# A hybrid decoder of two layers on one core: two buffers instead of one for the packed parameter tiles of a layer

## The chip, the cores and the metric

The kernel runs on one core of a Trainium2 chip. The core has a matrix engine (TensorE, PE in the rows), a vector engine (VectorE, DVE), an engine for activation functions (ScalarE, ACT), a general one (GpSimd, POOL) and SyncE (SP), which here issues every transfer between main memory and the core's own memory. Each engine runs its instructions in order and waits at semaphores for the others. The metric is the time of one execution on the device in microseconds (us): before the change the median of three runs is 938.91, from 938.29 to 939.07.

## The reference

x is 256 tokens of 1024 channels in float32; two layers follow each other, each with weights of its own.

```python
for l in range(2):
    h = rms_norm(x, g_mix)
    z = h @ w_in            # 1024 -> 6072 columns, split among three mixers and gates
    o_a = latent attention (8 heads, rotary on 32 dims)
    o_b = gated convolution of width 31 over 512 channels, layer norm, silu, projection
    o_c = sparse attention (8 heads, 2 key groups; compressed, selected and window branches)
    x = x + (sigmoid gates * (o_a, o_b, o_c) summed) @ w_out
    h = rms_norm(x, g_ffn)
    x = x + square(relu(h @ w_ff1)) @ w_ff2      # 1024 -> 4096 -> 1024
```

Besides its large matrices a layer has many small parameters: norm gains, biases, the 31 taps per channel of the convolution, gains of the rotary dims. They are what this change is about.

## The kernel before

The host packs a layer's small parameters into two arrays. cols (128 x 329 floats, 164.5 KB) holds what is used per partition: gains, biases, taps, two small matrices of the compressed branch. rows (128 x 192 floats, 96 KB) holds the gains of the rotary dims, repeated on every partition. layer(l) allocates a tile for each at its start (L256, L257) and loads both (L297, L298). Pools hand out such tiles by tag; with bufs=1 there is one slot per tag, and the tile of layer 1 is the slot of layer 0, so that the load of layer 1 waits until everything that reads layer 0's tile has done so.

The readers of rows are ten small products per rotary table on GpSimd (L305, L306: tqm, tkm, tqn, tkn, tkc, made once per layer, the last being tkcs). The readers of cols run through the whole layer, from hv on GpSimd (L318: five scaled copies) through the convolution (L758) to the gain of the second norm (L207, L208), shortly before the feed-forward part.

Weights stream. Each piece, 128 x up to 1024 floats (512 KB), lands in a slot raw, of which there are five (L138). ACT copies it to hi, a rounded float32r part (L153), and DVE subtracts to get lo (L154); hi and lo have rings of their own. Every product is then three matmuls: hi with hi, hi with lo, lo with hi (L163 to L165 with channels on the output's partitions, L171 to L173 with tokens there). A raw slot is free for a next load once its lo is made.

The start of layer 0 goes so: x, the identity, the norm's gains (gmix, into a raw slot as well), the constants cst, cols and rows are loaded, then wA0, the first part of w_in, in four pieces of 312 KB. The norm is computed for token block 0 (n1tx, transposes n1t, hh and hl), and then PE multiplies block 0 with wA0 (psA0, products of 312 columns, "part 0"), and after that with wA1 (psA1, four pieces, products of 512 columns, "part 1"). After the first product of part 1 PE transposes the norm of block 1. wA1's four pieces take the raw slots of wA0's four; the next weight, of wB, takes the slot of gmix, which DVE reads last for block 1 (n1tx, L220). kcv (L373) is ACT's copy of psA0's result.

The order of the instructions on each engine isn't that of the code. Steps get priorities (tc.cur_priority), and a scheduler places every instruction of both layers in its engine's queue by priority and by the time at which it thinks the instruction can run. So the loads of layer 1's cols and rows may stand in SyncE's queue in the midst of layer 0. The loads are given eight semaphores, "lanes", in turn; a load also waits for the load that had its lane before.

Of the kernel before, what the change touches and what calls it, by code (L numbers as in the profile page):

```python
# [16 lines left out]
P = 128  # L17
D = 1024
T = 256
# [12 lines left out]
# column offsets of the packed per-partition parameters  # L32
# [9 lines left out]
# row-broadcast gains of the rotary dims: [g, g with halves swapped]  # L42
# [16 lines left out]
# w_in: columns read with tokens on the output's partitions, then those with channels there  # L59
# [6 lines left out]
# the mixers' steps in the order of their data, and by urgency  # L66
# [19 lines left out]
def trunk_kernel(ctx: ExitStack, tc: tile.TileContext, A, out, depth=DEPTH):  # L86
# [54 lines left out]
    def piece(src, k, ring=0, half=0):  # L141
        """a piece [128, k, n] of a weight, split exactly into two float32r parts"""
        n = src.shape[-1]
        r = raw(src, n)
        if ring == 0:
            hi = wp.tile([P, 1024], R32, tag="hi", name="hi", bufs=WB)[:, :n]
            lo = wp.tile([P, 1024], R32, tag="lo", name="lo", bufs=WB)[:, :n]
        else:
            if half == 0:
                ring2[0] = (ap_.tile([P, 2048], R32, tag="big", name="hi2", bufs=BIG),  # L150
                            ap_.tile([P, 2048], R32, tag="big", name="lo2", bufs=BIG))
            hi, lo = (t[:, half * 1024:half * 1024 + n] for t in ring2[0])
        act(hi, r, AF.Copy)  # L153
        tt(out=lo, in0=r, in1=hi.bitcast(F32), op=ALU.subtract)  # L154
        return tuple(t.rearrange("p (k n) -> p k n", k=k) for t in (hi, lo))
# [3 lines left out]
    def gemm_b(ps, wh, wl, ah, al, ks, first=True, last=True):  # L159
        """ps[channel, token] += w^T a^T"""  # L160
        n = len(ks)
        for i, (kw, ka) in enumerate(ks):
            mm(ps, lhsT=wh(kw), rhs=ah(ka), start=(first and i == 0), stop=False)  # L163
            mm(ps, lhsT=wh(kw), rhs=al(ka), start=False, stop=False)  # L164
            mm(ps, lhsT=wl(kw), rhs=ah(ka), start=False, stop=(last and i == n - 1))  # L165

    def gemm_a(ps, ah, al, wh, wl, ks, first=True, last=True):
        """ps[token, channel] += a w"""
        n = len(ks)
        for i, (kw, ka) in enumerate(ks):  # L170
            mm(ps, lhsT=ah(ka), rhs=wh(kw), start=(first and i == 0), stop=False)  # L171
            mm(ps, lhsT=ah(ka), rhs=wl(kw), start=False, stop=False)  # L172
            mm(ps, lhsT=al(ka), rhs=wh(kw), start=False, stop=(last and i == n - 1))  # L173
# [5 lines left out]
    def rsqrt(v, p, n, name):  # L179
        """1/sqrt(v) of a positive [p, n] tile"""  # L180
        s = stat(n, name + "_s", I32)
        y = stat(n, name + "_y")
        h = stat(n, name + "_h")
        t = stat(n, name + "_t")
        s, y, h, t = s[:p], y[:p], h[:p], t[:p]
        ts(out=s, in0=v.bitcast(I32), scalar1=1, scalar2=None, op0=ALU.logical_shift_right)
        ts(out=h, in0=v, scalar1=-0.5, scalar2=None, op0=ALU.mult)
        ts(out=y.bitcast(I32), in0=s, scalar1=-1, scalar2=0x5f3759df, op0=ALU.mult, op1=ALU.add)
        for _ in range(3):
            if n == 1:  # L190
                ts(out=t, in0=y, scalar1=y, scalar2=h, op0=ALU.mult, op1=ALU.mult)
                ts(out=y, in0=t, scalar1=1.5, scalar2=y, op0=ALU.add, op1=ALU.mult)
            else:
                tt(out=t, in0=y, in1=y, op=ALU.mult)
                tt(out=t, in0=t, in1=h, op=ALU.mult)
                stt(out=y, in0=t, scalar=1.5, in1=y, op0=ALU.add, op1=ALU.mult)
        return y

    def transposed(src, b, g, hh, hl, name, c0):
        """columns c0 ... c0 + 3 (of 128) of src [128 tokens, 1024] -> block b of (src^T * g), split"""  # L200
        pt = psum("pt", name)
        for c in range(c0, c0 + 4):
            nc.tensor.transpose(pt[:, (c - c0) * P:(c - c0 + 1) * P], src[:, c * P:(c + 1) * P], ident)
        for c in range(c0, c0 + 4):
            pc = pt[:, (c - c0) * P:(c - c0 + 1) * P]
            hc = hh[:, c, b * P:(b + 1) * P]
            act(hc, pc, AF.Copy, scale=g[:, c:c + 1])  # L207
            stt(out=hl[:, c, b * P:(b + 1) * P], in0=pc, scalar=g[:, c:c + 1], in1=hc.bitcast(F32),  # L208
                op0=ALU.mult, op1=ALU.subtract)
# [5 lines left out]
    def normed(src, b, r, grow, hh, hl, name):  # L215
        """src [128 tokens, 1024] -> columns of block b of (src * r * g)^T, split"""
        for c0 in range(0, 8, 4):
            sl = slice(c0 * P, (c0 + 4) * P)
            xn = sp.tile([P, 512], F32, tag="s2", bufs=S2, name=name + "x")
            scaled[0] = stt(out=xn, in0=src[:, sl], scalar=r, in1=grow[:, sl], op0=ALU.mult, op1=ALU.mult)  # L220
            pt = psum("pt", name)
            for c in range(4):
                nc.tensor.transpose(pt[:, c * P:(c + 1) * P], xn[:, c * P:(c + 1) * P], ident)
            split(hh[:, c0:c0 + 4, b * P:(b + 1) * P], hl[:, c0:c0 + 4, b * P:(b + 1) * P],
                  pt.rearrange("p (c t) -> p c t", c=4))

    def sumsq_row(b, name, v):
        """mean square of x's rows in block b, plus eps"""
# [11 lines left out]
    def rope(X, n, half, ct, st, name, eng=None):  # L240
        """rotate the first 2*half columns of X [p, n, d] in place; ct, st [p, 2*half]"""
# [12 lines left out]
    def layer(l):  # L254
        last_layer = l == depth - 1
        cols = lp.tile([P, NCOL], F32, tag="cols", name="cols", bufs=1)  # L256
        rows = lp.tile([P, NROW], F32, tag="rows", name="rows", bufs=1)  # L257
# [27 lines left out]
        for b in range(NB):  # L285
            now = tc.cur_priority
            if l > 0 and b == 0:
                # block 0 goes before the last products of the block 1 of the layer before
                tc.cur_priority = tail_priority[0]
# [10 lines left out]
        # rotary tables times the gains of the rotated dims  # L300
# [20 lines left out]
        def part_a(i):  # L321
            """accumulators and weights; the products are added block by block"""
            return ([psum(t, "psA%d" % i) for t in (("at", "at"), ("po", "ch"), ("at", "at"))[i]],
                    [piece(A["wA%d" % i][l, kp], 2, ring=int(i == 1), half=kp % 2) for kp in range(4)])
# [7 lines left out]
        # channel-major part  # L332
        def take(*names):
            """one or two tiles, in one bank"""
# [21 lines left out]
        def a_products():  # L356
            """the first two parts; block 0 goes ahead"""
# [70 lines left out]
        def compress_kv():  # L428
# [13 lines left out]
            for xi, (wn, pe, w2) in enumerate((("ck1", "pek", "ck2"), ("cv1", "pev", "cv2"))):  # L442
# [11 lines left out]
                # four column groups of the array at a time; their sums are added by the next product  # L454
# [41 lines left out]
        def compress_scores():  # L496
            """all heads at once: order (block, pair, group, position)"""
# [31 lines left out]
        oh = ol = None  # L529

        def softmax_unit(pS, n, gate, name):
            """pS [128, n, keys] scores, a bank -> P^T [128 keys, 4 x 128 queries]"""
# [5 lines left out]
            # the negated masked scores and their minimum  # L538
# [24 lines left out]
        def nsa_attention(jp, o):  # L563
            """heads 2 jp, 2 jp + 1 of both groups"""
            po = psum("po", "nO")

            for b, js in ((0, (0, 1)), (1, (0,)), (1, (1,))):
# [3 lines left out]
                # the groups' products take turns: halves of the array that work at the same time  # L571
# [26 lines left out]
        def mla_attention(jp, o):  # L598
            """heads 4 jp ... 4 jp + 3"""
# [35 lines left out]
        def gemm32(ps, b, w, ks, c0, n):  # L635
            """ps[token, channel] = c_q or c_kv times w, a plain float32 product"""
# [6 lines left out]
        def low_rank_norm():  # L643
# [7 lines left out]
            # eps * (mean(c_q^2) + eps): per-token scale that the norm of c_q moves into the heads' norm  # L651
# [9 lines left out]
        def rotary_keys():  # L661
            krs = stat(2, "krs")
            # rotary part of the keys, shared by the heads
# [155 lines left out]
        def gated(m, c2):  # L819
            """column tiles 2 c2, 2 c2 + 1 of mixer m's projection, gated; the last of the three sums them"""  # L820
# [32 lines left out]
        def acc_pass(po4, held, ah, al, nk, b, ns=(0, 1)):  # L853
            """add the products of the held row tiles to the accumulators of token block b"""
# [23 lines left out]
        def ff1(gi):  # L878
            ps = psum("mm", "ff1")
            ws = [piece(A["ff1"][l, 2 * gi + u], 8) for u in range(2)]  # L880
            # the first group takes the channels in the order in which they arrive
# [48 lines left out]
def _lay(w, k, n):  # L930
    """[L, k*128, c*n] -> [L, c, 128, k*n]: chunks of n columns, contiguous per partition"""
# [4 lines left out]
def _rowsplit(w, k):  # L936
    """[L, K, n] -> [L, K/(128 k), 128, k*n]: chunks of k row tiles"""
# [118 lines left out]
```

## Time and profile before

| | |
|---|---|
| time, median of three runs | 938.91 us |
| the profiled execution's span, first to last instruction | 932.9 us |
| TensorE busy | 907.7 us (97%) |
| TensorE weight loads, beside the matmuls | 804.6 us (86%) |
| VectorE busy | 642.6 us (69%) |
| ScalarE busy | 538.4 us (58%) |
| GpSimd busy | 26.8 us (3%) |
| bytes moved | 151.55 MB, mean 162 GB/s |

The profile is one execution; the page gives its span but no time of its own from launch to end, so the median lies 6.0 us above the span (938.91 less 932.9) for what is around it. TensorE's busy time counts pipelined matmuls, so it isn't TensorE at its best; its gaps, though, are waits. The granted clock of TensorE has two levels, 1.2 and 2.4 GHz, and a mean of 1.00 in a stretch is 2.4 GHz throughout.

### The profile page before, as it was taken

The numbers are of one execution on the slowest core, as the hardware profiler recorded it, in microseconds if no ns is written. First come the engines' busy times: TensorE is split into PE (matmuls) and PEld (weight loads), VectorE is DVE, ScalarE is ACT, GpSimd is POOL, SyncE is SP. The second block draws the span as 40 slices with busy tenths as digits, with TensorE's granted clock in tenths as the row PEclk, the third lists the DMA queues.
The fourth block names the chain that finished last, engine by engine and source line by source line (L and its number), as shares of the span: only waits on it lengthen the run. The fifth ranks groups of instructions, "written<-read, shape, count | busy, mean of one in ns | idle before, by whom it ended". The sixth has DMA issues, their size and how long they took to land.

```text
span 932.9 us, 16104 instructions
## 1 busy us (share of the span) xinstructions
PE 907.7 (97%) x6214; PEld 804.6 (86%) x6214; DVE 642.6 (69%) x1431; ACT 538.4 (58%) x987; POOL 26.8 (3%) x80
## 2 busy tenths in 40 slices
PE   3999999999999999999999999999999999999998
PEld 3899888689989899999878988877999799999996
DVE  4589899775687655555476989979657785555552
ACT  3566656897456644444245575769865575444430
POOL 3210000000000000000001000000000000000000
PEclk9899999999999999999999999999999999999999
DMA  5644732224565665555444453225435476555521
GB/s 197 250 158 137 239 119 79 77 105 167 173 208 178 233 196 188 184 194 185 125 153 171 159 199 135 85 80 178 142 104 190 155 267 207 184 188 189 186 91 46
DMA packets 43133, 151.55 MB, mean 162 GB/s; under 512 B 4784, under 2 KB 5680, under 8 KB 43056
## 3 DMA queue, kind: packets, MB, share of 16 engines
q1 hardware_dynamic: 43056, 150.52, 48.2%
q8 instruction: 49, 0.80, 0.3%
q14 instruction: 28, 0.23, 0.1%
HBM read 149.45 MB, written 1.05 MB: 161 GB/s over the span
## 4 chain that ended last, share of the span: by engine, by line
PE 89%; DVE 4%; DMA 3%; ACT 2%; POOL 1%; issue 1%; SPq 0%; DVEq 0%; ACTq 0%
PE psB L163 7%; PE psB L165 7%; PE psB L164 7%; PE f L173 6%; PE f L171 6%; PE f L172 6%; PE ff L164 6%; PE ff L163 6%; PE ff L165 6%; PE wo L164 3%; PE wo L163 3%; PE wo L165 2%; PE nS L576 2%; DVE lo L154 2%; PE psA L172 2%; PE psA L171 2%
## 5 line engine op out<-in xcount | busy, mean ns | idle before, releaser
L154 DVE TENSOR_TENSOR lo<-raw,hi 128x1024 fp32r<-128x1024 f32 (+1 forms) x266 | 317.5, 1209 | 179.0 <-ACT hi L153 140.8
L153 ACT ACTIVATE hi<-raw 128x1024 fp32r<-128x1024 f32 (+1 forms) x266 | 274.7, 1048 | 267.2 <-DMA raw<-in_ff_dram 93.6
L163 PE MATMUL psB<-hh,hi 128*128 128x256 f32 x592 | 172.4, 292 | 1.4 <-ACT ug L749 1.4
L165 PE MATMUL psB<-hh,lo 128*128 128x256 f32 x592 | 170.2, 289 | 0.0
L164 PE MATMUL psB<-hl,hi 128*128 128x256 f32 x592 | 169.5, 287 | 0.0
L165 PE MATMUL ff<-h,lo 128*128 128x256 f32 x512 | 144.5, 283 | 0.0
L163 PE MATMUL ff<-h,hi 128*128 128x256 f32 x512 | 144.5, 283 | 0.0
L164 PE MATMUL ff<-l,hi 128*128 128x256 f32 x512 | 144.3, 283 | 0.0
L163 PEld LDWEIGHTS psB<-hh,hi 128*128 128x128 f32 x592 | 113.1, 191 | 8.2 <-issue 4.4
L165 PEld LDWEIGHTS psB<-hh,lo 128*128 128x128 f32 x592 | 112.8, 191 | 3.0 <-issue 2.6
L164 PEld LDWEIGHTS psB<-hl,hi 128*128 128x128 f32 x592 | 113.1, 191 | 0.3
L758 DVE SCALAR_TENSOR_TENSOR ca<-upad,cols,ca 128x256 f32<-128x256 f32 x240 | 103.6, 477 | 0.4
L173 PE MATMUL f<-hi,rl 128*128 128x512 f32 x256 | 101.2, 395 | 0.5 <-DVE rl L892 0.5
L171 PE MATMUL f<-hi,rh 128*128 128x512 f32 x256 | 101.1, 395 | 0.0
L172 PE MATMUL f<-lo,rh 128*128 128x512 f32 x256 | 101.0, 395 | 0.0
L164 PEld LDWEIGHTS ff<-l,hi 128*128 128x128 f32 x512 | 98.0, 192 | 1.1
L163 PEld LDWEIGHTS ff<-h,hi 128*128 128x128 f32 x512 | 97.9, 191 | 1.2
L165 PEld LDWEIGHTS ff<-h,lo 128*128 128x128 f32 x512 | 98.0, 192 | 0.0
L173 PEld LDWEIGHTS f<-hi,rl 128*128 128x128 f32 x256 | 48.0, 188 | 13.0 <-DVE rl L892 1.6
L171 PEld LDWEIGHTS f<-hi,rh 128*128 128x128 f32 x256 | 48.1, 188 | 10.2
L172 PEld LDWEIGHTS f<-lo,rh 128*128 128x128 f32 x256 | 48.0, 188 | 10.3
L171 PE MATMUL psA<-hi,hh 128*128 128x512 f32 (+1 forms) x96 | 36.4, 381 | 6.9 <-ACT hi L153 6.9
(279 smaller groups left out, 1425.1 us busy)
## 6 DMA issues: line engine op xcount, KB each, us to landing
raw<-in_ff_dram SPq DMA_DIRECT2D x128, 512.0 KB, 4.0
raw<-in_wB_dram SPq DMA_DIRECT2D x74, 512.0 KB, 4.0
raw<-in_wA_dram SPq DMA_DIRECT2D x16, 512.0 KB, 4.4
raw<-in_w_out_dram SPq DMA_DIRECT2D x16, 512.0 KB, 3.5
raw<-in_wo_nsa_dram SPq DMA_DIRECT2D x8, 512.0 KB, 4.8
raw<-in_wo_mla_dram SPq DMA_DIRECT2D x8, 512.0 KB, 4.0
raw<-in_wconv_dram SPq DMA_DIRECT2D x8, 512.0 KB, 3.7
raw<-in_wA_dram SPq DMA_DIRECT2D x8, 312.0 KB, 5.3
```

Of the source, the lines that this page charges most:

```text
L153: act(hi, r, AF.Copy)
L154: tt(out=lo, in0=r, in1=hi.bitcast(F32), op=ALU.subtract)
L163: mm(ps, lhsT=wh(kw), rhs=ah(ka), start=(first and i == 0), stop=False)
L164: mm(ps, lhsT=wh(kw), rhs=al(ka), start=False, stop=False)
L165: mm(ps, lhsT=wl(kw), rhs=ah(ka), start=False, stop=(last and i == n - 1))
L171: mm(ps, lhsT=ah(ka), rhs=wh(kw), start=(first and i == 0), stop=False)
L172: mm(ps, lhsT=ah(ka), rhs=wl(kw), start=False, stop=False)
L173: mm(ps, lhsT=al(ka), rhs=wh(kw), start=False, stop=(last and i == n - 1))
L576: mm(pS[g].rearrange("p (h z k) -> p h z k", h=nj, z=2)[:, i], lhsT=qTn[gs, 2 * jp + j, b * P:(b + 1) * P], rhs=kTn[gs, :, 0:nk], start=Tr ...
L758: stt(out=ca[:, i], in0=upad[:, i, k:k + T], scalar=K("wdw", 31 * i + k), in1=ca[:, i], op0=ALU.mult, op1=ALU.add)
```

## The change

Both tiles get two buffers. The rest of the diff takes out comments and leaves the line numbers as they are.

```diff
     def layer(l):
         last_layer = l == depth - 1
-        cols = lp.tile([P, NCOL], F32, tag="cols", name="cols", bufs=1)
-        rows = lp.tile([P, NROW], F32, tag="rows", name="rows", bufs=1)
+        cols = lp.tile([P, NCOL], F32, tag="cols", name="cols", bufs=2)
+        rows = lp.tile([P, NROW], F32, tag="rows", name="rows", bufs=2)
```

With that the scheduler places some instructions elsewhere. SyncE's queue at the start of layer 0, before (the number behind a name tells tiles apart: rows_5141 is layer 1's, raw_219 to raw_237 hold wA0; what a load waits for stands in brackets, where DMAHW0 to 7 are the lanes, Pool, DVE and Activation are engines, and _49 is the same everywhere):

```order
L138 DMA raw_219<-in_wA0_dram 128x624
L138 DMA raw_225<-in_wA0_dram 128x624 [waits DMAHW0_49]
L138 DMA raw_231<-in_wA0_dram 128x624 [waits DMAHW1_49]
L138 DMA raw_237<-in_wA0_dram 128x624 [waits DMAHW2_49]
L298 DMA rows_5141<-in_rows_dram 128x192 [waits DMAHW6_49,DMAHW3_49,Pool_49]
L138 DMA raw_245<-in_wA1_dram 128x1024 [waits DMAHW7_49,DMAHW4_49,DVE_49]
```

and the same place now (cols_5140 is layer 1's):

```order
L138 DMA raw_219<-in_wA0_dram 128x624
L138 DMA raw_225<-in_wA0_dram 128x624 [waits DMAHW0_49]
L138 DMA raw_231<-in_wA0_dram 128x624 [waits DMAHW1_49]
L138 DMA raw_237<-in_wA0_dram 128x624 [waits DMAHW2_49]
L297 DMA cols_5140<-in_cols_dram 128x329 [waits DMAHW3_49]
L298 DMA rows_5141<-in_rows_dram 128x192 [waits DMAHW4_49]
L138 DMA raw_245<-in_wA1_dram 128x1024 [waits DMAHW7_49,DMAHW5_49,DVE_49]
```

The load of layer 1's cols has come to stand here, and that of its rows no longer waits for GpSimd, nor for the landing of layer 0's rows. Lane 3 is that of gmix, lane 4 that of the constants. SyncE's queue in the feed-forward part of layer 0, as a difference:

```order
 L138 DMA raw<-in_w_out_dram 128x1024 x8
-L138 DMA raw<-in_ff_dram 128x1024 x11
-L297 DMA cols<-in_cols_dram 128x329
-L138 DMA raw<-in_ff_dram 128x1024 x53
+L138 DMA raw<-in_ff_dram 128x1024 x64
 L138 DMA raw<-in_gmix_dram 128x1024
```

The load of layer 1's cols is gone from here. GpSimd's queue, at the end of layer 1's tables:

```order
 L306 TENSOR_TENSOR tqms<-cst,rows 128x32 x2
-L745 MEMSET upad 128x4x30
 L318 TENSOR_SCALAR hv<-cols 128x8
 L318 TENSOR_SCALAR hv<-cols 128x4 x2
 L318 TENSOR_SCALAR hv<-cols 128x1 x2
+L745 MEMSET upad 128x4x30
```

Layer 1's hv now stands ahead of the memset of the convolution's padding. The queues of TensorE, VectorE and ScalarE hold the same instructions in the same order as before.

## Rows read from the trace of the kernel before

**Rows 1.** The first line of the page and TensorE's line of part 1: the span, and busy us, share of the span and instructions.
```profile
span 932.9 us, 16104 instructions
...
PE 907.7 (97%) x6214; PEld 804.6 (86%) x6214; DVE 642.6 (69%) x1431; ACT 538.4 (58%) x987; POOL 26.8 (3%) x80
```

**Rows 2.** The table by stretch: from:to and length in us, then busy us and instructions of each engine, TensorE's granted clock as a share of 2.4 GHz, the mean busy share of the 16 DMA engines, and GB/s. A stretch of idle time has a clock of its own that means little.
```profile
18.70:24.69 5.99, 0.22 (x3) 0.01 (x1) 0.02 (x1) 1.11 (x2) 0.00 (x1) 0.72 0.78 276
24.69:28.67 3.98, 3.98 (x15) 3.47 (x15) 3.65 (x4) 3.42 (x6) 0.00 (x0) 0.57 0.96 367
28.67:62.00 33.33, 32.85 (x188) 28.97 (x187) 20.55 (x43) 17.02 (x27) 4.84 (x16) 1.00 0.57 194
...
278.00:306.00 28.00, 27.48 (x174) 24.07 (x173) 19.83 (x35) 18.32 (x35) 1.62 (x5) 1.00 0.58 194
...
733.00:761.00 28.00, 27.99 (x176) 24.51 (x175) 20.57 (x35) 18.99 (x38) 0.00 (x0) 1.00 0.58 202
```

**Rows 3.** The chain of waits from 18 to 30 us, in order of time: start us, us that the piece takes on the chain, what it is (DMA is a transfer from its issue to its landing, SPq is SyncE's queue issuing it, PE is TensorE).
```profile
17.86 0.67 POOL tkcc L305
...
18.73 0.33 SPq L298
...
19.17 4.39 DMA raw<-in_wA_dram
...
23.58 1.06 ACT hi L153
...
24.69 0.79 PE psA L171
25.48 1.71 PE n1t L223 x8
```

**Rows 4.** SyncE's own queue from 0 to 62 us: waiting line <- what it waited for: us in total, times, longest us.
```profile
SPq L298 <- POOL tkcs L306: 8.3, 1, 8.3
```

**Rows 5.** SyncE's issues from 0 to 62 us in order of time: start us, us, engine, line, operation, out<-in, count (a count above one covers several issues and the waits between them).
```profile
2.59 0.43 SPq L296 DMA_DIRECT2D cst<-in_cst_dram  x1
...
21.11 5.14 SPq L138 DMA_DIRECT2D raw<-in_wB_dram  x2
```

**Rows 6.** DMA issues that start from 0 to 18.7 us: out<-in, queue, operation, count, KB each, median us from issue to landing.
```profile
raw<-in_wA_dram SPq DMA_DIRECT2D x4, 312.0 KB, 7.4
x<-in_x_dram SPq DMA_DIRECT2D x2, 512.0 KB, 4.0
...
cst<-in_cst_dram SPq DMA_DIRECT2D x1, 276.0 KB, 7.1
```

**Rows 7.** VectorE (DVE) from 0 to 62 us in order of time; in brackets the idle time before and what ended it.
```profile
9.14 1.41 DVE L220 SCALAR_TENSOR_TENSOR n1tx<-x,n_y,raw 128x512 f32<-128x512 f32 x2 [0.78 <-DMA raw<-in_gmix_dram]
...
12.40 0.80 DVE L154 TENSOR_TENSOR lo<-raw,hi 128x624 fp32r<-128x624 f32 x1
...
14.02 0.80 DVE L154 TENSOR_TENSOR lo<-raw,hi 128x624 fp32r<-128x624 f32 x1
...
17.03 1.41 DVE L220 SCALAR_TENSOR_TENSOR n1tx<-x,n_y,raw 128x512 f32<-128x512 f32 x2
24.67 1.23 DVE L154 TENSOR_TENSOR lo<-raw,hi 128x1024 fp32r<-128x1024 f32 x1 [6.23 <-ACT hi L153]
...
27.24 1.31 DVE L177 TENSOR_TENSOR hl<-n1t,hh 128x512 fp32r<-128x512 f32 x2
```

**Rows 8.** TensorE (PE) from 18 to 32 us in order of time: one matmul a line, with its start and its length from first to last step (matmuls overlap, so the next one's start tells the pace).
```profile
18.46 0.31 PE L172 MATMUL psA<-lo,hh 128*128 128x312 f32 x1
18.61 0.30 PE L173 MATMUL psA<-hi,hl 128*128 128x312 f32 x1
...
28.67 0.39 PE L171 MATMUL psA<-hi,hh 128*128 128x512 f32 x1
28.90 0.39 PE L172 MATMUL psA<-lo,hh 128*128 128x512 f32 x1
...
31.27 0.40 PE L172 MATMUL psA<-lo,hh 128*128 128x512 f32 x1
```

**Rows 9.** The chain of waits from 480 to 490 us, where layer 1 does the same transposes.
```profile
486.52 0.45 PE n1t L223 x4
```

**Rows 10.** ScalarE (ACT) from 0 to 62 us in order of time.
```profile
24.54 0.58 ACT L373 ACTIVATE kcv<-psA 128x512 f32<-128x512 f32 x1
25.02 1.05 ACT L153 ACTIVATE hi<-raw 128x1024 fp32r<-128x1024 f32 x1
...
31.33 1.06 ACT L153 ACTIVATE hi<-raw 128x1024 fp32r<-128x1024 f32 x1 [1.61 <-PE psA L173]
```

**Rows 11.** Around the first feed-forward weights of layer 0 (some 290 to 312 us) and of layer 1 (745 to 767 us): a load on the chain of layer 0, one on the chain of layer 1, two of SyncE's issues in layer 0, and for the five loads issued from 745 to 755 us their us from issue to landing.
```profile
295.57 5.18 DMA raw<-in_ff_dram
...
748.99 4.13 DMA raw<-in_ff_dram
...
298.01 0.33 SPq L297 DMA_DIRECT2D cols<-in_cols_dram  x1
300.96 10.05 SPq L138 DMA_DIRECT2D raw<-in_ff_dram  x6
...
DMA to landing us min/median/max: 3.9/4.2/5.0
```

**Rows 12.** ScalarE from 505 to 540 us: its first read of hv in layer 1.
```profile
514.42 0.46 ACT L748 ACTIVATE ua<-psB,hv 128x256 f32<-128x256 f32 x1
```

## The prediction

> **What bounds the kernel now.** I read the page's busy shares first: TensorE (PE) works 907.7 of 932.9 us [rows 1], so at most 25.2 us of waiting can go, plus what its matmuls lose at the lower clock. The table by stretch says where [rows 2]. From 18.70 to 24.69 PE works 0.22 us of 5.99. From 24.69 to 28.67 it is full, but at a granted clock of 0.57 (a mix of 1.2 and 2.4 GHz). From 28.67 to 62 it works 32.85 of 33.33 us at 1.00.
>
> The chain of waits, read backwards from PE's restart, names the cause of that hole [rows 3]: the product of 24.69 waits for ACT's hi (23.58, 1.06 us), that for a transfer of wA1 issued at 19.17 (4.39 us), that for SP's own L298 at 18.73, and that for POOL's last tables of layer 0. SP's queue view agrees: L298 waited 8.3 us for tkcs [rows 4]. This L298 is the load of layer 1's rows. With one buffer it may not land before POOL has read layer 0's rows, and SP, which issues in order, holds the wA1 loads behind it.
>
> **The change, step 1: the hole at 18.7 us.** By the order above, cols and rows of layer 1 now go out as twelfth and thirteenth transfer and wait for lanes alone: rows for the constants, issued at 2.59 [rows 5] and landed 7.1 us later [rows 6], at 9.7; cols for the norm's gains, which had landed when DVE used them at 9.14 [rows 7]. So both are out by about 10.5 us, and SP stands at the first wA1 load. That load takes the slot of the first wA0 piece and waits for its lo: 12.40 + 0.80 = 13.20 on DVE [rows 7]. The second goes at 14.02 + 0.80 = 14.82, the third and fourth before DVE's n1tx of 17.03, the next weight (wB) at 17.03 + 1.41 = 18.44.
>
> Landing of the first piece: 4.39 us is this very transfer in the chain, with three more right behind it; the ends are 4.0 us (x, into an empty queue) and 7.4 us (wA0 behind 2 MB of other loads) [rows 6]. I take 4.39: at 13.2 us the wA0 burst has nearly landed. The 260.5 KB of the two new loads cost 0.7 us of transfer at the 367 GB/s of the third stretch in [rows 2], and are through before wA1's data start. So 13.25 + 4.39 = 17.64; hi until 18.70; PE's last product of part 0 starts at 18.61 and the next may follow 0.14 us later, at 18.75 [rows 8]. There is practically no hole: the restart moves from 24.69 to 18.75, 5.94 us.
>
> Then the clock. Before, PE fell from 2.4 to 1.2 GHz in the hole: its product of 24.69 takes 0.79 us, the same product at 28.67, back at 2.4 GHz, 0.39 [rows 3, 8]. With gaps of about 0.5 us it does not fall: the stretch of 278 to 306 has 0.52 us of idle time and a clock of 1.00 [rows 2]. So I count the next products at full clock: one at 0.23 us; eight transposes at two times 0.48 (four take 0.45 us on layer 1's chain, [rows 9]) instead of 1.71 [rows 3], until 19.94. The next product needs lo of the first piece, 1.23 us on DVE [rows 7]: 18.70 + 0.04 + 1.23 = 19.97. Five products of 0.23 end the piece at 21.1; before, the second piece began at 28.67 [rows 8], 7.5 us later.
>
> From here DVE and ACT are what is late. ACT's kcv waits for the end of part 0's block 0 (18.61 + 0.30 = 18.91); the second hi starts 0.48 us after kcv [rows 10], 19.43 to 20.48; its lo 20.53 to 21.76. So the second piece's L172 product runs at 21.8 in place of 28.90: 7.1 us. The check one step on: hh of block 1 and the third hi are done on ACT by 22.4 (0.48 between starts, then 1.05); DVE does two hl (1.31) and lo of the third piece by 24.15; PE wants that at 21.8 + 5 x 0.23 + 0.23 + 7 x 0.14 = 24.2, where before it was 31.27. Again 7.1, with 0.05 us to spare.
>
> Do later loads keep up with a PE that is 7.1 us earlier? The first wB piece is issued at 18.47 in place of 21.11 [rows 5] and lands by 23; ACT took it at 31.33 after a wait for PE [rows 10], so it is wanted at 24.2. The others are issued when lo of an earlier piece is done, which moves by the same 5 to 7 us. The stretch from 28.67 has only 0.48 us of PE idle time, so nothing there was waiting on transfers, and the shift is carried to the end. Step 1: -7.1 us, between -7.5 (no lateness of DVE) and -2.6 (landing after 7.4 us: 20.65, hi 21.71, PE 21.76, 2.9 us earlier, less 0.3 us of lateness behind it).
>
> **Step 2: cols at 298 us.** Before, layer 1's cols were issued at 298.01, among the first feed-forward weights [rows 11]. SP's next load, at 300.96, had its own wait for a slot. But the weight in flight took 5.18 us on the chain, where the chain's load in layer 1 took 4.13, and PE idled 0.52 us of 28 there against 0.01 in layer 1 [rows 2, 11]. So the gain is between 0 (loads there land in 3.9 to 5.0 us without any cols, so 5.18 may be scatter) and 0.5 (all of it goes). I take 0.3.
>
> A rule of the Trainium skill bears on this: "DMA: Bandwidth & Descriptors", section "Queues, rings and completion order", says that each transfer engine consumes a queue's descriptors in ring order. By it cols, issued 2.4 us behind the weight on the same queue, could not hold it up, and step 2 would be 0; by the row of 5.18 us it is up to 0.5. The total would be 931.8 by the rule and 931.3 by the row.
>
> **Step 3: the rest.** hv of layer 1 (five POOL instructions) is no longer held until cols land at about 302 and goes ahead of the memset of upad. Its first reader is ACT at 514.42 [rows 12], so 200 us cover both. The later transfers each use the next lane; a lane's earlier transfer is eight back, while five raw slots limit what is in flight. Cost 0. PE, DVE and ACT run the same instructions in the same order.
>
> Sum: the profiled execution's span of 932.9 goes to 932.9 - 7.1 - 0.3 = 925.5. The median of the timed runs, 938.91, lies 6.0 us above that span; this part outside the span is untouched, so **931.5 us**.
>
> **Rivals.**
> - The loads land late. For it: wA0's 7.4 us in this same corner of the kernel. Against it: that burst had 2 MB ahead of it, and here the queue is empty but for 260 KB. The restart then comes 2.9 us earlier and the lateness costs 0.3: 938.9 - 2.6 - 0.3 = 936.0.
> - The hole closes, but PE's clock drops all the same, in the wait of 0.7 us (21.1 to 21.8) for the second piece's lo. For it: the clock has risen only shortly before, in the last products of part 0. Against it: 0.52 us of idle time at clock 1.00. Then the restart's 5.9 us remain: 938.9 - 5.9 - 0.3 = 932.7.
> - The wait moves on: wB or wA2 arrive too late for the earlier PE, and by 62 us nearly all is given back. For it: five raw slots, and transfer engines busy to 0.96 from 24.69 to 28.67. Against it: from there to 62 us they are busy to 0.57 only [rows 2]. Only step 2 is left: 938.6.
> - Slower: the clock drops in that same wait and does not come back while the loads run close behind PE, each short wait keeping it at 1.2 GHz. Work that takes 1 us at 2.4 GHz then takes 2; it decides once 7.4 us of such work runs at the low clock, and all of the stretch to 62 us would add 32.9: 964. Against it: before, after a far longer hole, the clock was back within 4 us [rows 8], and 0.48 us of idle time later did not move it.
>
> **How the numbers follow.** Chances: forecast 0.74, late loads 0.11, clock drop 0.09, wait moved on 0.03, slower 0.03. The first three are faster by more than 0.2% (1.9 us, about what a measurement of this kernel can tell from no change): 0.94. Low end 930.6: 7.5 and 0.5 off 938.9 is 930.9, less 0.3 for the spread of the timed runs. High end 934.5: it holds the clock drop and a landing up to some 2.5 us late, and leaves out the worst of the late loads and the last two cases.
>
> **What would show it.** Right: SP issues wA1 at about 13.3; PE's gap after 18.9 shrinks from 5.8 us to under 0.3; the clock reads about 1.00 from 18.7 to 28; PE's gap of 0.5 us near 304 (297 then) is gone; the same sequence 7.1 us earlier up to 278. Wrong: a new wait of PE for hi or lo between 19 and 40 us of more than 1 us, or a shift that shrinks between 30 and 62 us.

## The result and the profile after

The changed kernel took **928.82 us** (median of 6 runs, 928.34 to 932.83) against 937.77 us of the kernel before on the same chip (6 runs, 936.10 to 939.07): a ratio of 0.992, 95% interval 0.9902 to 0.9939. Faster was right, and 931.5 / 938.91 is 0.992 too. But the time lies 1.8 us under the low end of the range, 930.6, and both the level and the spread have to be explained.

The profiled execution of the changed kernel took 932.83 us, the slowest of its six. First line and TensorE's line of the page, for [rows 1]:

```profile
span 930.9 us, 16102 instructions
...
PE 909.1 (98%) x6214; PEld 805.4 (87%) x6214; DVE 642.6 (69%) x1431; ACT 538.4 (58%) x987; POOL 27.2 (3%) x80
```

SyncE's issues, as in [rows 5]: layer 1's rows go out at 9.62 us and no longer wait for GpSimd, and the four wA1 loads start at 13.21, where 13.25 was forecast.

```profile
9.62 0.33 SPq L298 DMA_DIRECT2D rows<-in_rows_dram  x1
13.21 3.69 SPq L138 DMA_DIRECT2D raw<-in_wA_dram  x4
18.46 1.49 SPq L138 DMA_DIRECT2D raw<-in_wB_dram  x2
```

TensorE in order of time, as in [rows 8]. Part 0 ends at 17.71 and part 1 follows at 17.85 without a gap. The two waits that are left, 0.44 and 0.46 us, end with lo on VectorE.

```profile
17.71 0.30 PE L173 MATMUL psA<-hi,hl 128*128 128x312 f32 x1
17.85 0.40 PE L171 MATMUL psA<-hi,hh 128*128 128x512 f32 x1
18.09 1.11 PE L223 MATMUL n1t<-cst,n1tx 128*128 128x128 f32 x8
19.64 0.51 PE L172 MATMUL psA<-lo,hh 128*128 128x512 f32 x1 [0.44 <-DVE lo L154]
...
21.78 0.50 PE L172 MATMUL psA<-lo,hh 128*128 128x512 f32 x1 [0.46 <-DVE lo L154]
...
24.27 0.40 PE L172 MATMUL psA<-lo,hh 128*128 128x512 f32 x1
```

The last of these is the product that stood at 31.27 [rows 8]: 7.00 us earlier. The chain of waits, as in [rows 3], tells what is late now: the second wA1 piece lands at 19.38 and gives hi, lo and the product of 21.78.

```profile
14.83 4.55 DMA raw<-in_wA_dram
19.41 1.07 ACT hi L153
20.50 1.24 DVE lo L154
21.78 0.50 PE psA L172
```

The table by stretch, with the columns of [rows 2]. The hole has gone (5.09 of 5.99 us busy, before 0.22) and the clock is 1.00 behind it. But 62 to 278 us reads 0.98, and at the start of layer 1's feed-forward part, from 733 us, TensorE now idles 0.95 us where it idled 0.01 [rows 2]:

```profile
18.70:24.69 5.99, 5.09 (x25) 3.92 (x25) 5.08 (x6) 4.28 (x6) 0.00 (x0) 1.00 0.98 367
24.69:28.67 3.98, 3.98 (x24) 3.56 (x24) 1.83 (x3) 1.73 (x3) 1.93 (x5) 1.00 0.93 280
28.67:62.00 33.33, 32.85 (x208) 29.50 (x207) 23.74 (x55) 18.84 (x31) 7.86 (x19) 1.00 0.55 175
62.00:278.00 216.00, 215.13 (x1620) 189.07 (x1619) 173.34 (x500) 145.23 (x322) 4.36 (x13) 0.98 0.43 143
278.00:306.00 28.00, 27.36 (x169) 24.07 (x168) 21.03 (x36) 21.22 (x38) 0.00 (x0) 1.00 0.57 188
...
733.00:761.00 28.00, 27.05 (x166) 23.57 (x165) 20.30 (x36) 20.13 (x38) 0.00 (x0) 1.00 0.55 179
```

A finer table of that stretch, of TensorE alone (length, busy us and count, granted clock, DMA share, GB/s), finds it: for 6.6 us TensorE works without a gap at a granted clock of 0.50, 1.2 GHz, and loses 3.3 us.

```profile
84.00:88.00 4.00, 4.00 (x36) 1.00 0.10 24
88.00:91.00 3.00, 3.00 (x21) 1.00 0.76 243
91.00:97.60 6.60, 6.60 (x31) 0.50 0.97 361
```

The profile of the kernel before had nothing of the kind there. So the gain of 7.0 us that stands at 30 us has shrunk to 3.9 us by the first cS products (126.5 us before, 122.6 now) in these two profiles, and ends at 2.0 us (932.9 to 930.9), while the timed runs differ by 8 to 9. That contradiction is what the experiments had to settle.

### The profile page after: what moved, and what is told of

Read it like the earlier page. It is cut to its first block, busy times and chain, and to the rows that moved or that the text cites. A ratio compares the mean times of both kernels' runs of the same rounds, so it can differ in the third digit from the quotient of the medians.

```text
span 930.9 us, 16102 instructions
## 1 busy us (share of the span) xinstructions
PE 909.1 (98%) x6214; PEld 805.4 (87%) x6214; DVE 642.6 (69%) x1431; ACT 538.4 (58%) x987; POOL 27.2 (3%) x80
## 4 chain that ended last, share of the span: by engine, by line
PE 86%; DVE 6%; DMA 4%; ACT 2%; issue 1%; SPq 0%; DVEq 0%; ACTq 0%
PE psB L163 7%; PE psB L165 7%; PE psB L164 7%; PE f L173 6%; PE f L171 6%; PE f L172 6%; PE ff L164 6%; PE ff L163 6%; PE ff L165 6%; DVE lo L154 3%; PE wo L164 2%; PE wo L163 2%; PE wo L165 2%; PE nS L576 2%; PE uq L638 2%; PE psA L172 2%
## 5 line engine op out<-in xcount | busy, mean ns | idle before, releaser
L172 PE MATMUL f<-lo,rh 128*128 128x512 f32 x256 | 101.0, 395 | 0.0
L172 PEld LDWEIGHTS f<-lo,rh 128*128 128x128 f32 x256 | 48.0, 188 | 10.3
L172 PE MATMUL psA<-lo,hh 128*128 128x512 f32 (+1 forms) x96 | 36.0, 375 | 2.1 <-DVE lo L154 2.1
```

## The experiments

Two accounts of the level stood against each other. One: some 2 us lie outside the span, the hole is worth the forecast 7 us in every run, and the runs differ by other stretches at the lower clock, inside the span. The rival, as predicted: 6 us lie outside the span in every run. Apart from that: which half of the change works, and by what?

**The kernel before, again.** No edit.

> The kernel before, unchanged, to see span and granted clock of every timed run. The profiled execution before had a span of 932.9 us and a clock of 0.996, the changed kernel's runs are 1.9 us longer than their spans. Theory A (the outside part is 1.9 us here too, and the timed runs before are longer inside, by stretches at 1.2 GHz that the profiled execution did not have): spans of 934 to 937 us, clocks of 0.989 to 0.995, lower for the longer runs. Rival B (the outside part is 6 us, as the prediction took it): spans of 930 to 933 us at 0.996, whatever the time.

Measured: 937.32 us (12 runs, 934.03 to 941.24), ratio 0.9995 (0.9975 to 1.0014). Time less span, which is all that can lie outside, is 1.8 to 2.2 us in every run. The spans themselves go from 932.0 to 939.2, and a longer span comes with a lower mean clock: 0.996 at 932.0, 0.990 at 939.2. A run at 1.2 GHz for t us of full work loses t/2, and its mean clock falls by t/2 over the span, so the loss should be about 930 x (1 - clock). Over 35 runs of the kernel before (these 12 and 23 beside them) a straight line through the spans has a slope of 899 and starts at 930.3 us; single runs lie up to 2.5 us off it (standard deviation 1.0). With the 36 runs of the same kernel beside the later experiments the line has 788 and 930.9, so the rule is a rough one. But 2 us lie outside in every run, and the rest is in the span: the prediction's account falls. The profile of this run shows such a stretch behind a group of cS products, first in TensorE's order of time, then in its table by stretch:

```profile
125.27 1.12 PE L576 MATMUL nS<-kTn,qTn 64*128 64x512 f32 x2
126.32 1.97 PE L502 MATMUL cS<-kbd,qTn 128*128 128x32 f32 x16
128.13 0.54 PE L163 MATMUL psB<-hh,hi 128*128 128x256 f32 x1
128.47 0.42 PE L164 MATMUL psB<-hl,hi 128*128 128x256 f32 x1
```

```profile
127.00:128.00 1.00, 1.00 (x11) 1.00 0.00 0
128.00:129.00 1.00, 1.00 (x7) 0.58 0.05 8
129.00:130.00 1.00, 1.00 (x7) 0.50 0.57 217
130.00:131.00 1.00, 1.00 (x6) 0.50 0.80 315
131.00:132.00 1.00, 1.00 (x9) 0.71 0.81 184
```

**Rows alone: the kernel before with two buffers for rows.**

```diff
-        rows = lp.tile([P, NROW], F32, tag="rows", name="rows", bufs=1)
+        rows = lp.tile([P, NROW], F32, tag="rows", name="rows", bufs=2)
```

> Only rows gets a second buffer; cols keeps one. Theory A (the hole at 18.7 us is the wait of layer 1's rows load for GpSimd, and nothing else of the change counts): as fast as the whole change, 928 to 932 us, first product of part 1 at about 17.9 us in the profile. Rival C (the early load of cols, or its absence at 298 us, brings a part): 1 us or more slower than the whole change.

Measured: 931.34 us (4 runs, 927.57 to 932.37), ratio 0.9921 (0.9891 to 0.9951). The hole is gone: the rows' buffer alone removes it. The table by stretch of this run and of the next two, in their order, from 18.70 to 24.69 us:

```profile
18.70:24.69 5.99, 5.60 (x32) 4.61 (x31) 4.96 (x6) 4.76 (x7) 0.88 (x1) 1.00 1.00 375
18.70:24.69 5.99, 1.05 (x5) 0.80 (x5) 0.41 (x1) 1.50 (x3) 0.08 (x1) 0.79 0.79 277
18.70:24.69 5.99, 5.59 (x32) 4.62 (x31) 4.82 (x6) 4.57 (x7) 0.00 (x0) 1.00 0.97 360
```

The median lies 2.5 us above the changed kernel's, as rival C asked for, but the intervals of the two ratios nearly coincide (0.9891 to 0.9951 here, 0.9902 to 0.9939 there), so four runs don't decide on rival C. In this profile the feed-forward weight that was in flight when cols were issued took 7.34 us to land, and the stretch from 278 to 306 us has TensorE at 25.59 of 28 us. The chain of waits:

```profile
288.56 7.34 DMA raw<-in_ff_dram
295.92 1.06 ACT hi L153
```

**Cols alone: the kernel before with two buffers for cols.**

```diff
-        cols = lp.tile([P, NCOL], F32, tag="cols", name="cols", bufs=1)
+        cols = lp.tile([P, NCOL], F32, tag="cols", name="cols", bufs=2)
```

> Only cols gets a second buffer; rows keeps one, so that its load still waits for GpSimd's tables. Theory A: no gain, ratio 0.999 to 1.001, the hole of 5.8 us at 18.7 us is there. Rival C: 1 us or more faster.

Measured: 936.37 us (10 runs, 933.87 to 941.47), ratio 0.9986 (0.9966 to 1.0007), with the hole in place (second row above). No change that can be told from none.

**One buffer each, but another place in the queue.** Layer 1's rows load stands behind the last gate weight of layer 0 in SyncE's queue (it goes out at 187.48 us); the load of cols stays among the feed-forward weights (291.26 us). The lines that keep hold of the weight's load are left out of the diff.

```diff
-        nc.sync.dma_start(out=rows, in_=A["rows"][l])
+        if l == 0:
+            nc.sync.dma_start(out=rows, in_=A["rows"][l])
+        else:
+            with tc.issue_after(load[1].ins):
+                nc.sync.dma_start(out=rows, in_=A["rows"][l])
```

> One buffer for both tiles, but the load of layer 1's rows is held in SyncE's queue until after the last gate weight of layer 0, so that it stands behind the wA1 loads. Theory A (what costs is the place in the queue, not the buffer): as fast as the whole change, 928 to 932 us, no hole at 18.7 us. Rival D (the second buffer helps in some way of its own): near the time of before, 936 to 938 us.

Measured: 929.45 us (4 runs, 928.86 to 934.10), ratio 0.9919 (0.9888 to 0.9950), without the hole (third row above). Without a byte of extra buffer it does what the change does. So the loss was never the missing buffer as such: it was a load with a long wait that stood ahead of urgent ones in a queue that issues in order.

**The changed kernel, again.** No edit.

> The changed kernel once more, unedited, to see how its times and granted clocks spread. Over the 35 timed runs of the kernel before, the span goes as 930.1 us + 930 us x (1 - mean granted clock), within 1.1 us; the six runs of the changed kernel go as 926.4 + 930 x (1 - clock). Theory (stretches at the lower clock fall on both kernels alike, beside the hole's own): median 928.5 to 931.5 us, ratio 0.990 to 0.994, mean clock 0.997 to 0.999, spans on the 926.4 line within 1.1 us, time minus span 1.7 to 2.2 us. Rival (the first six runs drew a good lot): mean clock at 0.995 to 0.996 and a median of 932 to 933.5 us.

Measured: 928.93 us (6 runs, 927.49 to 930.97), ratio 0.9912 (0.9886 to 0.9937), mean clock 0.9992, time less span 1.9 to 2.1. The first six runs were no lucky draw.

**The hole kept, but filled.** The kernel before, with 21 products into a spare bank behind part 0's first block. The condition around these lines (layer 0, block 0, the step of part 1) and the line that remembers the last product of part 0 are left out of the diff.

```diff
+                        with tc.issue_after(tl0[0].ins):
+                            fill = psum("mm", "fill")
+                            for k in range(21):
+                                tl0[0] = mm(fill.rearrange("p (c t) -> p c t", c=4), lhsT=hh[:, k % 8, 0:P],
+                                             rhs=hh[:, 0:4, 0:P], start=(k == 0), stop=(k == 20))
+                        with tc.issue_after(tl0[0].ins):
+                            add_a(i, pa01[i], b)
```

> The kernel before with its hole kept, but with 21 products of 512 columns (hh by hh, into a bank that nothing reads) put on TensorE behind the last product of the first gate piece, about 5 us of work, so that the engine is not idle while layer 1's rows load holds the queue; the 8 transposes n1t then stand among them. Their result is used by nothing. Theory (the hole is a wait of 5.8 us and, behind it, 4 us at the lower clock): wA1's hi still ends near 24.6 us, the granted clock from 24.69 to 28.67 is 1.00 instead of 0.50, and the gain is 1.0 to 2.0 us (3.98 us of work halves, but the lo subtractions on VectorE come at 25.9, 27.3 and about 29.8): ratio 0.998 to 0.999, mean clock higher by 0.003 to 0.004. Rival 1 (the clock is worth nothing here, VectorE's lo sets the pace anyway): 0, ratio 0.9995 to 1.0005. Rival 2 (the lower clock is half of the gain of the change, as the difference of the mean clocks, 0.004 of 930 us, would have it): 3.5 to 4 us, ratio 0.996.

Measured: 934.70 us (12 runs, 933.68 to 939.93), ratio 0.9977 (0.9958 to 0.9997), that is 2.2 us, just above what the theory gave. The ends of the interval touch both rivals, 0.9995 and 0.996, so the times alone rule out neither. The trace is sharper. The clock stays at 1.00 where it was 0.72 and 0.57 [rows 2]:

```profile
18.70:24.69 5.99, 5.23 (x24) 3.82 (x22) 1.22 (x1) 2.31 (x3) 0.00 (x0) 1.00 0.84 314
24.69:28.67 3.98, 3.23 (x13) 2.25 (x14) 3.78 (x6) 3.05 (x5) 0.00 (x0) 1.00 1.03 393
```

The transposes qTn_p, the first work that both kernels do in the same order again, begin at 60.8 us in the kernel before, at 59.2 in the filled one, at 53.8 in the changed one (name, count, min/median/max ns, first and last start):

```profile
L416 PE MATMUL qTn_p<-cst,qn x8: 272/273/309, 60.8 to 63.3; 128*128 128x128 f32 x8
```

```profile
L426 PE MATMUL qTn_p<-cst,qn x8: 272/273/300, 59.2 to 61.7; 128*128 128x128 f32 x8
```

```profile
L416 PE MATMUL qTn_p<-cst,qn x8: 272/273/301, 53.8 to 56.3; 128*128 128x128 f32 x8
```

So of the 7.0 us, about 1.6 come back by keeping the clock up (with the eight n1t, which the filler let move into the hole, counted in), and 5.4 are the wait itself. These are single profiles: the other two with the hole begin the transposes at 60.6 (kernel before, again) and 61.1 (cols alone), the six others without it at 53.6 to 54.1, so the hole is worth 6.5 to 7.5 and the clock's part of it 1.4 to 1.9. And wA1's first hi begins at 22.38 in the filled kernel, where it began at 23.58 before [rows 3]. That counts for little: the kernel before, again, has TensorE's restart as early (23.43, filled 23.50) and is only 0.2 us earlier at the transposes. TensorE's order of time in the filled kernel shows why the clock gives no more: at full speed it waits for lo instead.

```profile
19.08 4.35 PE L372 MATMUL fill<-hh 128*128 128x512 f32 x18
23.50 0.50 PE L172 MATMUL psA<-hi,hh 128*128 128x512 f32 x1
24.75 0.51 PE L173 MATMUL psA<-lo,hh 128*128 128x512 f32 x1 [0.76 <-DVE lo L154]
...
28.51 0.50 PE L173 MATMUL psA<-lo,hh 128*128 128x512 f32 x1 [0.69 <-DVE lo L154]
```

**Where the other low stretches come from.** In the changed kernel's profile the stretch began 2 us behind twelve css products of one column; in the run of the kernel before above, and from 582.3 us in the filled one, behind the cS products of 32. Three edits of the changed kernel try these places.

css over 128 columns instead of one (the lines that read one of the 128 copies are left out):

```diff
-                        mm(pss[:, o + b:o + b + 1], lhsT=sqs[i][:, b * P:(b + 1) * P], rhs=ones[:, 0:1],
+                        mm(pss[:, (o + b) * P:(o + b + 1) * P], lhsT=sqs[i][:, b * P:(b + 1) * P], rhs=ones,
```

> The changed kernel with the column sums css taken as products of 128 columns instead of one (the same sums, written 128 times side by side, of which one is read). In the profile of the changed kernel the granted clock is 0.50 from 91.0 to 97.6 us, right behind the twelve one-column css products at 87.6 us, with TensorE busy without a gap. Theory (products of one column count for little as activity, and the clock falls behind them): no stretch at 0.50 near 91 us, and timed runs with a mean clock of 0.999 or more in at least 5 of 6, span 926 to 928 us. Rival (the fall comes from something else, DMA load or nothing of this core's): mean clocks spread from 0.994 to 1.000 as in the changed kernel, whose mean is 0.998. The order on three engines moves by some rows, so the time may differ by a microsecond either way; the clocks are what is read.

Measured: 942.33 us (10 runs, 940.30 to 944.58), ratio 1.0055. The theory falls as stated: only one of ten runs has a clock above 0.998. (The profiled run is that one and has no low stretch, so it shows nothing of where the others fell.) The time grew by 13 us at much the same clock. By the page's waits the order that moved has a price of its own, of which one line shows a part (0.3 us in the changed kernel):

```profile
PE nT L555 <- ACT nP L550: 3.6, 4, 1.5
```

The cS group three times over:

```diff
-            for b in range(NB):
+            for b in list(range(NB)) * 3:
```

> The changed kernel with the group of cS products (8 products of 32 columns, 16 rows and 1.97 us in the trace) issued three times over in each layer, the first two results overwritten. Two profiles so far show the granted clock at 0.50 for about 3 us right behind this group (from 128.3 us in a run of the kernel before, from 582.4 us in the filled one) with TensorE busy; most show it at 1.00 there. Theory (the group is what the fall follows): with 6 us of it the clock falls behind it in both layers in nearly every run: mean clock lower than the changed kernel's 0.999 by 0.003 to 0.004 or more, a stretch at 0.50 behind both groups in the profile, time 928.9 + 2 x 3.9 of work + 2 x 1.7 to 3.3 us = 940 to 943 us. Rival (the place is chance, or follows something else): mean clock 0.998 to 0.999 and 936 to 938 us. The order behind it moves by some rows, up to 2 us either way; the clocks decide.

Measured: 956.49 us (4 runs), ratio 1.0196 (1.0148 to 1.0244), mean clocks 0.985 to 0.993. The profile has a long stretch at 0.50 in both layers, from inside the group on; the table of TensorE:

```profile
116.00:120.00 4.00, 4.00 (x28) 1.00 0.00 0
120.00:124.00 4.00, 4.00 (x31) 0.80 0.43 131
124.00:128.00 4.00, 4.00 (x21) 0.50 0.00 0
128.00:132.00 4.00, 4.00 (x20) 0.50 0.41 135
...
592.00:596.00 4.00, 4.00 (x28) 0.68 0.37 131
596.00:600.00 4.00, 4.00 (x20) 0.50 0.00 0
600.00:604.00 4.00, 4.00 (x21) 0.54 0.42 131
```

So the fall follows this group when it is three times as long, in all four runs by their clocks. That the single group of 2 us brings it on too, in some runs and not in others, is argued from its place and not shown. The time is 13 us above the upper end of what was expected; that excess was not taken apart and stays open.

cS over 64 columns instead of 32 (the line that reads one of the two copies is left out):

```diff
-                    mm(pS[:, o:o + 32], lhsT=qTn[:, j, b * P:(b + 1) * P], rhs=kbd, start=True, stop=True)
+                    mm(pS[:, o:o + 64].rearrange("p (r c) -> p r c", r=2), lhsT=qTn[:, j, b * P:(b + 1) * P],
+                       rhs=bc(kbd.rearrange("p (o c) -> p o c", o=1), [P, 2, 32]), start=True, stop=True)
```

> The changed kernel with the cS products over 64 columns instead of 32 (the same 32 columns written twice, one copy is read). Theory (the fall follows this group because its products are so narrow): no stretch at 0.50 behind it, mean clock of the timed runs 0.999 to 1.000 in all but one. Rival (it follows something else): clocks spread as in the changed kernel, 0.996 to 1.000. Time 928 to 931 us by either, since the order on three engines moves by some rows; if the stretches go and the order costs nothing it is the fastest so far, 927 to 928 us.

Measured: 935.32 us (10 runs), ratio 0.9983 (0.9963 to 1.0003), clocks 0.996 to 1.000, four of ten below 0.999: the rival's spread, not the theory's. The profile has no fall behind cS, but one behind css, in TensorE's order of time and in its table:

```profile
546.85 1.39 PE L650 MATMUL css<-ones,csq 128*128 128x1 f32 x12
548.17 1.12 PE L577 MATMUL nS<-kTn,qTn 64*128 64x512 f32 x2
...
550.61 0.42 PE L165 MATMUL psB<-hh,lo 128*128 128x256 f32 x1
```

```profile
551.00:552.00 1.00, 1.00 (x8) 0.50 0.98 352
```

Neither place alone accounts for the spread, and this version is 6 us slower than the changed kernel at much the same clock. No version beats the changed kernel. Widening both groups was not tried.

## Why the prediction was right about the change and wrong about the time

| runs | us, median | mean clock | span less 930 x (1 - clock), mean us |
|---|---|---|---|
| kernel before, 35 | 937.62 | 0.9940 | 930.1 |
| cols alone, 10 | 936.37 | 0.9949 | 930.0 |
| before, hole filled, 12 | 934.70 | 0.9982 | 931.8 |
| rows later, 4 | 929.45 | 0.9975 | 926.2 |
| rows alone, 4 | 931.34 | 0.9985 | 927.2 |
| changed kernel, 12 | 928.87 | 0.9988 | 926.4 |

**Step 1, the hole: right up to 62 us.** wA1's first issue 13.21 (forecast 13.25), restart of TensorE 17.85 (18.75), the second piece's L172 at 21.78 (21.8), the third's at 24.27 (24.2). The gaps after 18.9 are 0.44 and 0.46 us, above the 0.3 that was to show it. The shift is 7.00 us where 7.1 was forecast, and until 62 us it does not shrink. Two errors cancel: TensorE came to full clock earlier than in the profile before, at 15.9 us instead of 17.7, so part 0 ended 0.9 us sooner, and that went into waits for lo, which set the pace as foreseen. That was luck of this profile: the moment lies between 15.5 and 18.8 us in the eleven profiles, and at 18.6 in the second one of the changed kernel, whose shift at the transposes qTn_p is 6.7 us. The rows alone give the shift, the place in the queue alone gives it. "The shift is carried to the end" held less well: at the start of layer 1's feed-forward part, from 733 to 765 us, TensorE idles 0.6 to 0.95 us in the four profiles of the change or of its rows half (changed kernel twice, rows alone, rows later) and 0.0 to 0.2 in the three with the hole unfilled, so about half a microsecond is given back there.

**Step 2, cols: not seen.** 0.3 us was taken; TensorE idles 0.64 us from 278 to 306 against 0.52 before, so the gap that was to go is still there, and cols alone have one of 0.72 us at 305.86 without any cols near. That layer 1 had next to no gap in the profile before (0.01 us) was no sign of what cols cost in layer 0 either: with the change it has 0.95. Cols alone come out at 0.9986 with 1 inside the interval. The weight in flight landed after 5.18, 6.17, 7.34, 5.54 and 5.09 us where cols were issued behind it (the kernel before twice, rows alone, rows later, hole filled). Four profiles without cols there (two of the changed kernel, css wide, cS wide) have 5.29, 5.60, 5.62 and 6.58 on the chain; in the other two, cols alone and cS three times, the longest load there takes 5.7 and 4.8. The ranges overlap, so the gain of step 2 stays open. The rule of the Trainium skill that was weighed here ("DMA: Bandwidth & Descriptors", "Queues, rings and completion order") is neither borne out nor refuted by them; the page states the order in which descriptors are consumed, and that cols behind a weight could not hold it up was the prediction's own step from there.

**Step 3: right as far as it shows.** No new wait appears at hv, and none between 28.67 and 62 us (32.85 us busy in both).

**The step that failed is the last one of the sum:** "The median of the timed runs, 938.91, lies 6.0 us above that span; this part outside the span is untouched". What lies outside is 1.7 to 2.2 us in each of the 137 runs that have a span on record. The three runs behind 938.91 and the profiled execution have no such pair of numbers; by 1.9 us the latter took about 934.8, less than any of the six runs beside it (936.10 at least). So the other 4 us are, by the later runs of the same kernel, time inside the span, most of it low-clock stretches that the profiled execution, at 932.9 among the shortest (7 of 71 spans are no longer), happened not to have. Held at 6.0, the term measured 3.4 in the changed kernel (928.87 - 925.5). With the right term the span forecast, 925.5, gives 927.5 for a run without such stretches. The shortest of the twelve took 927.49, with a clock of 1.000, but that is the best of four runs at this clock, whose spans go up to 927.0.

The error hid two things. First, the three runs of the time before were a draw from a spread of 934 to 941 us: 35 runs have their median at 937.6, 1.3 us lower. Second, "0.3 for the spread of the timed runs" was far too little for a range that starts from it. The remaining 1.3 us is gain: medians 8.75 us apart, means 8.3, against 7.4 forecast (six of the twelve ran on another chip than the 35; the kernel before has medians of 937.10 and 937.07 on the two other chips).

By the table, 3.7 us is the difference at equal clock and 4.5 that of the clocks (0.0048 x 930), in which the idle time of the hole at low clock is counted with the rest. The low clock in and behind the hole comes to 3.4 us of these 4.5 in each of the three profiles that have it (before: 0.28 x 5.99 + 0.43 x 3.98), so the hole is worth about 7.1 us by the timed runs too. The last 1.1 us would be fewer chance stretches in the changed kernel; with a standard error of 0.5 us that stays open.

**The rivals.** Late loads: no, 3.4 and 4.55 us for the first two pieces. Clock drop in the wait for lo: no, 1.00 through waits of 0.44 and 0.46. Wait moves on: not by 62 us, and only about half a microsecond later. Slower by a clock that stays low: not there; but the mechanism it named, TensorE at 1.2 GHz while it has work, is real at other places, and most of what the 6.0 us had wrong.

## What to carry to other kernels

Read an in-order issuing queue for the load that waits longest and ask what stands behind it: here a second buffer and a later place for that one load were worth the same (0.992 of the time each). Measure time less span before counting anything as outside the span, and compare a profile with timed runs only at equal mean clock. A profile is one draw: with two levels of clock, 930 x (1 - clock) tells roughly, to 1 us or so, what each run of this kernel lost to it.

## What the runs showed of the hardware that was not expected

TensorE fell to 1.2 GHz while it was busy without a gap in the trace, in some runs and not in others: 6.6 us from 91.0 (changed kernel), about 3.4 us from 128.2 (before, again), about 3.4 us from 582.3 (filled), some 6.8 us from 550.4 (cS over 64 columns). Each began within 2.3 us of the end of a group of products of 1 or 32 columns, with two nS products beside it, and where the group of 32 columns lasted some 8 us it was there in both layers. The Trainium skill ("TensorE: Matmul & The Clock Gate", "HAM oscillation — how this bites in real kernels") tells of such falls behind waits of TensorE. The hole is one (5.8 us of idle time, 0.57 behind it [rows 2]); these rows show falls without a wait, and none behind the waits of about 0.5 us. The same groups also pass at 1.00 (the first profile of the kernel before, 91 to 97.6 and 128 to 132 us), so what decides in a given run is open. Transfers are no common sign: the DMA share was 0.00 to 0.05 when the clock fell at 128.2.

At the start of the kernel the clock column misses the lower level. From 13.7 us to the moment named under step 1 a product of 312 columns follows the last after 0.26 us, behind it after 0.14, and the column reads 1.00 throughout. So a mean of 1.00 isn't 2.4 GHz throughout there, as was said of such a mean ahead of the prediction, and the mean clocks of the table leave this stretch out.
